# RWKV heads in pairs on whole 128x128 tiles, half of the rate products on GpSimd, and a repeated list schedule with due dates

## The chip, the core and the metric

The kernel runs on one core of a Trainium2 chip. TensorE (PE, with PEld for its weight loads), VectorE (DVE), ScalarE (ACT), GpSimd (POOL) and SyncE (SP, which issues the DMAs) each take their own instructions in order and meet through semaphores. The metric is the device time of one execution in microseconds, the median of several runs.

## The reference

Two layers on 512 positions of 1024 channels, then a final norm. Each layer projects the normed input and feeds three branches: a gated linear recurrence with a short convolution (RG-LRU), an RWKV-7 recurrence with 16 heads of 64 channels, and a retention. The branches are projected back, gated, summed and added to the input. The change is in the RWKV branch, whose core is this recurrence over positions:

```python
kk = kk / jnp.maximum(jnp.linalg.norm(kk, axis=-1, keepdims=True), 1e-12)
k = k * (1.0 + (a - 1.0) * k_a)
def step(state, inp):
    r_t, w_t, k_t, v_t, kk_t, a_t = inp
    sa = jnp.einsum("bhvk,bhk->bhv", state, -kk_t)
    state = (state * w_t[:, :, None, :]
             + sa[..., None] * (kk_t * a_t)[:, :, None, :]
             + v_t[..., None] * k_t[:, :, None, :])
    y = jnp.einsum("bhvk,bhk->bhv", state, r_t)
    return state, y
y = head_norm(y, RWKV_GN_EPS).reshape(bsz, s, W_B) * lnx_w + lnx_b
bonus = (jnp.sum(rh * kh * r_k, axis=-1, keepdims=True) * vh).reshape(bsz, s, W_B)
return (y + bonus) * jax.nn.silu(g)
```

## The kernel before

Channels lie on the 128 partitions, the 512 positions in the columns. A projection (`proj`, L502) streams 282 weight tiles of 128x1024 from HBM (`raw`, 512 KB each). ACT rounds a tile to fp32r (`whi`), DVE makes the remainder (`wlo`), and the product is three matmuls for each of eight slices of the contraction: 24 records named `acc` of 128x128 weights and 512 columns. PSUM buffers of `acc` are freed by the ACT and DVE instructions that read them out.

RWKV works on four groups in each layer, one group being two tiles of 128 channels, that is four heads. For a group, `rwkv_prep` (L749) makes the decays and `rwkv_scores` (L791) the rest: decayed copies of the keys and rates (`ar`, `bk`), the 64x64 products of a chunk with itself (`sc`, one head on a 64-row tile), which DVE masks into `E`. Then a forward elimination on POOL inverts 32x32 triangles (`ex`, `etmp`, 62 instructions of up to 64x256); its input comes by DMA (`ead`) and its result goes out by DMA (`exd`), is transposed by DVE (`xn`), and PE makes the remaining quarter of each inverse (`w`, 32x32 tiles). `vt` are the values transposed, `pcp` the chunk decays.

`rwkv_chain` (L913) goes through eight chunks of 64 positions in turn. A step is a hop from PE to ACT or DVE and back, three times: `p` from the state `sv` (64 columns, weights `ar` and `stk`), copied to `zs` by ACT; `p` from `zs` with weights `E`, copied to `sv`; `p` from `sv` with `tbk`, to which DVE adds the decayed old state (`dec`, made on POOL). All of these are 64x64 or 128x64 tiles. `stk` is `ar` and `E` moved across the partitions by DMA, 256 KB each. `rwkv_out` (L953) norms the result and transposes it back (`yt`).

Nothing is issued where it is written. `Scheduler` records every instruction with a price in us and the tiles it reads and writes, `run` makes a list schedule over the engines from these prices, priorities and free buffers, and then issues in that order. So all rows of the profile have line 318, and work is told apart by its tiles, out<-in. Tiles come from pools with a fixed number of buffers; `etmp`, `sgb`, `g`, `bonus` and `lraw` share the pool `tc` with seven.

## Time and profile before

| | us |
|---|---|
| median of three runs | 2125.97 |
| the runs | 2125.53, 2125.97, 4809.5 |
| span of the profiled execution | 2125.0 |
| PE busy | 2082.5 (98%) |
| DVE busy | 1145.0 (54%) |
| ACT busy | 914.6 (43%) |
| POOL busy | 415.0 (20%) |

The profile is of one execution, whose span is its own time. PE's busy time counts overlapping matmuls once; what one matmul costs is read from one start to the next, since matmuls are pipelined and their ends modelled. PE made 12204 records, DVE 1605 instructions, ACT 1384, POOL 590. The granted clock of PE was 0.9 or more of full speed in nearly all of 40 slices of the span.

### The profile page before, as it was taken

Reading aid. Unit: us, or ns where it says so; the run is one execution under the profiler, and the core shown is the slowest. Engines: PE = TensorE matmul, PEld = TensorE weight load, DVE = VectorE, ACT = ScalarE, POOL = GpSimd, SP = SyncE. Lnnn points to the kernel's source line nnn. Section 1 sums busy time; section 2 is a strip of 40 time slices with the busy share of each in tenths; the row PEclk is TensorE's granted clock in tenths of the full one; section 3 lists DMA queues with packets and bytes.
Section 4 is the critical chain, followed back from the end, with each engine's and each line's share of the span. In section 5 each row is a group of like instructions: output and inputs, shape, how many; then the busy total and the mean of one; then the engine's idle time right before and its main releaser. Section 6 shows DMA issues by size and latency. Waiting matters only on the chain.

```text
span 2125.0 us, 30185 instructions
## 1 busy us (share of the span) xinstructions
PE 2082.5 (98%) x12204; PEld 1648.6 (78%) x12204; DVE 1145.0 (54%) x1605; ACT 914.6 (43%) x1384; POOL 415.0 (20%) x590
## 2 busy tenths in 40 slices
PE   7999999999999999999999999999999999999996
PEld 5777788787788777888877777787887787788884
DVE  8764584474448524344568546644744555253433
ACT  5754652534442424232456466425344424242333
POOL 1062107005200800000010801251070035100000
PEclk9999999999999999999999999999999999999998
DMA  4332242123214323243524212421431243142441
GB/s 161 102 110 63 76 133 89 50 95 102 80 47 128 115 74 124 95 139 99 175 76 131 87 54 92 124 85 54 111 97 55 75 117 122 50 147 92 139 139 60
DMA packets 103147, 210.63 MB, mean 99 GB/s; under 512 B 42848, under 2 KB 44128, under 8 KB 103008
## 3 DMA queue, kind: packets, MB, share of 16 engines
q1 hardware_dynamic: 103008, 208.71, 31.5%
q8 instruction: 96, 1.57, 0.3%
q14 instruction: 43, 0.35, 0.1%
HBM read 175.11 MB, written 20.97 MB: 92 GB/s over the span
## 4 chain that ended last, share of the span: by engine, by line
PE 88%; POOL 5%; DVE 2%; DMA 1%; ACT 1%; issue 1%; SPq 0%; DVEq 0%; ACTq 0%; POOLq 0%
PE acc L318 61%; PE p L318 8%; PE vp L318 5%; PE sc L318 3%; POOL etmp L318 3%; POOL ex L318 3%; PE gate L318 2%; PE w L318 2%; PE rsc L318 2%; PE rout L318 2%; PE lora L318 1%; PE vt L318 1%; PE kss L318 1%; PE tr L318 1%; PE bps L318 1%
## 5 line engine op out<-in xcount | busy, mean ns | idle before, releaser
L318 PE MATMUL acc<-hh,whi 128*128 128x512 f32 x1504 | 621.2, 413 | 2.4 <-DVE q L318 2.4
L318 PE MATMUL acc<-hl,whi 128*128 128x512 f32 x1504 | 590.7, 393 | 3.7 <-DVE hl L318 2.4
L318 PE MATMUL acc<-hh,wlo 128*128 128x512 f32 x1504 | 590.7, 393 | 0.8 <-DVE wlo L318 0.6
L318 DVE TENSOR_TENSOR wlo<-raw,whi 128x1024 fp32r<-128x1024 f32 x282 | 357.7, 1268 | 313.9 <-ACT whi L318 312.2
L318 ACT ACTIVATE whi<-raw 128x1024 fp32r<-128x1024 f32 x282 | 298.0, 1057 | 519.7 <-PE acc L318 367.0
L318 PEld LDWEIGHTS acc<-hh,whi 128*128 128x128 f32 x1504 | 284.0, 189 | 78.7 <-issue 12.3
L318 PEld LDWEIGHTS acc<-hh,wlo 128*128 128x128 f32 x1504 | 284.0, 189 | 64.2 <-DVE wlo L318 2.3
L318 PEld LDWEIGHTS acc<-hl,whi 128*128 128x128 f32 x1504 | 284.7, 189 | 60.2 <-issue 3.4
L318 POOL TENSOR_TENSOR etmp<-ex,ea 64x31 f32<-64x31 f32 (+15 forms) x248 | 169.1, 682 | 131.7 <-DMA ea<-ead 85.4
L318 POOL TENSOR_TENSOR ex<-ex,etmp 64x31 f32<-64x31 f32 (+15 forms) x248 | 167.0, 674 | 19.4
L318 POOL TENSOR_TENSOR dec<-sv,pc 64x256 f32<-64x256 f32 x48 | 51.7, 1077 | 473.1 <-DVE sv L318 473.1
L318 ACT ACT_TABLE_LOAD x87 | 111.6, 1283 | 2.2 <-PEq L1202 0.7
L318 PE MATMUL acc<-yh,whi 128*128 128x512 f32 x256 | 103.0, 402 | 0.0
L318 PE MATMUL acc<-ylo,whi 128*128 128x512 f32 x256 | 100.5, 393 | 0.0
L318 PE MATMUL acc<-yh,wlo 128*128 128x512 f32 x256 | 99.8, 390 | 0.0
L318 ACT ACTIVATE thm<-acc,der 128x512 f32<-128x512 f32 x48 | 33.0, 687 | 137.7 <-PE acc L318 136.9
L318 PE MATMUL acc<-mq,whi 128*128 128x512 f32 x256 | 79.3, 391 | 0.0
L318 PE MATMUL acc<-yq,whi 128*128 128x512 f32 x256 | 78.9, 389 | 0.0
L318 PE MATMUL vp<-whi,hh 128*128 128x256 f32 x256 | 77.7, 304 | 0.0
L318 ACT ACTIVATE zs<-p 64x256 f32<-64x256 f32 x64 | 24.1, 377 | 119.6 <-PE p L318 119.2
L318 POOL TENSOR_TENSOR hl<-hf,hh 128x512 fp32r<-128x512 f32 x8 | 12.8, 1601 | 311.7 <-ACT hh L318 311.7
L318 DVE TENSOR_TENSOR sv<-p,pc 64x256 f32<-64x256 f32 x56 | 23.3, 417 | 93.2 <-PE p L318 79.6
(208 smaller groups left out, 3193.5 us busy)
## 6 DMA issues: line engine op xcount, KB each, us to landing
raw<-in_w SPq DMA_DIRECT2D x282, 512.0 KB, 3.3
yl<-ys SPq DMA_DIRECT2D x48, 256.0 KB, 4.9
stk<-ar SPq DMA_DIRECT2D x16, 256.0 KB, 4.7
ar<-E SPq DMA_DIRECT2D x16, 256.0 KB, 3.0
stk<-E SPq DMA_DIRECT2D x16, 256.0 KB, 3.0
ys<-thg SPq DMA_DIRECT2D x16, 256.0 KB, 2.9
ys<-bonus SPq DMA_DIRECT2D x16, 256.0 KB, 2.3
ys<-yr SPq DMA_DIRECT2D x16, 256.0 KB, 2.6
```

The lines of the kernel that those rows point to most:

```text
L318: fn(*[r(v) for v in pos], **{k: r(v) for k, v in kw.items()})
```

## The change

Two heads share a whole 128x128 tile, one in each half of the partitions, and zeros fill the rest. The score factors become `se` and `so`, the triangles `xd` (both heads on the diagonal) and `br`, the state update `tb`; a chain step has 4 + 2 + 2 + 2 products, with one head's columns in each half of the rows of `sv` and `zs`. The copies of a hop are split, half 0 on ACT and half 1 on DVE. The decay of a chunk is multiplied into `bk` ahead of its transposes, so `pcp` and the moves `stk` are gone. `vt` is made of fp32r halves, `yt` is a product with a constant instead of a transpose, `lraw` is padded to 128 rows, and `w` uses 128x128 weights. Of the rate products, `r * pp` and `k * pi` go to POOL in 64 half products of 64x512; 136 fills with zeros go there too. `raw` has two buffers instead of three, `whi` three instead of two.

The scheduler gets new prices, twelve rounds, and due dates: after a round, the date by which each instruction must start so that PE is not held up, worked back from the round's own times, is the priority in the next; the shortest round is issued. Buffers of the PSUM pools `a` and `d` may be taken out of the recorded order. An argument `claims` is handed through, and emptied where an instruction is committed.

```diff
--- before.py
+++ after.py
-    caps = {"h": 16, "tp": 16, "tc": 7, "tm": 13, "q": 12, "sv": 1, "raw": 3, "whi": 2, "wlo": 2,
-            "zs": 2, "sn": 2, "pc": 2, "ssq": 2, "vm": 2}
+    caps = {"h": 16, "tp": 16, "tc": 7, "tm": 13, "q": 12, "sv": 1, "raw": 2, "whi": 3, "wlo": 2,
+            "zs": 2, "sn": 2, "pc": 2, "ssq": 2, "vm": 2, "vv": 2}
+    S.loose = {"a", "d"}
...
+    def _set_due(self):
+        for op in sorted(self.ops, key=lambda o: (-o.start, -o.i)):
+            due = op.start if op.eng == "PE" or not op.succ else math.inf
+            for s in op.succ:
+                due = min(due, s.due - op.cost - LATENCY[op.eng] * (not s.eng == op.eng == "PE"))
...
+            x = x[:8] + ((),)
...
+    def run(self, rounds=12):
+        for op in self.ops:
+            op.left, op.due = op.ndep, None
+        best = None
+        for _ in range(rounds):
+            length = self._schedule()
+            if best is None or length < best[0]:
+                best = length, sorted(self.ops, key=lambda o: (o.start, o.i))
+            self._set_due()
+        order = best[1]
...
-        c = 0.095 + out.size / 1200.0
+        c = 0.18 + out.size / 1200.0
...
-        S.rec("DVE", nc.vector.tensor_tensor, 0.07 + out.size / 960.0, dict(out=out, in0=in0, in1=in1, op=op))
+        S.rec("DVE", nc.vector.tensor_tensor, 0.15 + out.size / 960.0, dict(out=out, in0=in0, in1=in1, op=op))
...
-    def mm(out, lhsT, rhs, start, stop, n, check=True):
...
-        cost = n / 2400.0 + 0.0025 if fast else max(n, lhsT.size) * 4 / 2400.0
-        if out.box[0]:
-            cost = 0.04
-        S.rec("PE", nc.tensor.matmul, cost, kw, pos=(out,))
+        cost = (n + 32) / 2400.0 if fast else (4 * max(n, 64) + 26) / 2400.0
+        S.rec("PE", nc.tensor.matmul, cost, kw, pos=(out,), claims=claims)
 
     def transpose(out, in_, ident):
-        S.rec("PE", nc.tensor.transpose, 0.06, {}, pos=(out, in_, ident))
+        S.rec("PE", nc.tensor.transpose, 0.109, {}, pos=(out, in_, ident))
...
+        raw = tl("tc", "lraw", [P, 2, 256])
+        memset("POOL", raw[HK:P, 0], 0.0)
+        memset("POOL", raw[0:HK, 1], 0.0)
+        dma(raw[0:HK, 0], wt[l, W_LORA][0:HK, g * 256:(g + 1) * 256], HK * 1024)
+        dma(raw[HK:P, 1], wt[l, W_LORA][HK:P, g * 256:(g + 1) * 256], HK * 1024)
...
-            tt(A[:, :, 0, 1:], c3(kn[:])[:, :, 1:], c3(pp[:])[:, :, :CH - 1], ALU.mult)
-            tt(A[:, :, 1, :], c3(r[i][:]), c3(pp[:]), ALU.mult)
+            for s_, A in enumerate((se, so)):
+                rr = half(s_)
+                stt(A[rr, :, s_, 1:], c3(kn[:])[rr, :, 1:], 2.0, c3(pp[:])[rr, :, :CH - 1], ALU.mult, ALU.mult)
+                ts(A[rr, :, s_, 0:1], c3(kn[:])[rr, :, 0:1], 2.0, None, ALU.mult)
+                ptt(A[rr, :, 1 - s_, :], c3(r[i][:])[rr], c3(pp[:])[rr], ALU.mult)
...
-            tt(B[:, :, 1, :], c3(k[i][:]), c3(pi[:]), ALU.mult)
+            for s_ in range(2):
+                rr = half(s_)
+                tt(B[rr, :, s_, :], c3(kn[:])[rr], c3(pi[:])[rr], ALU.mult)
+                ptt(B[rr, :, 1 - s_, :], c3(k[i][:])[rr], c3(pi[:])[rr], ALU.mult)
...
-                            mm(ps[:, c4, :], B[rr, c].rearrange("p a s -> p (a s)"),
-                               A[rr, c].rearrange("p a s -> p (a s)"), True, True, P)
-                    tt(e[:, 4 * half:4 * half + 4, :], ps[:], mask_s.unsqueeze(1).to_broadcast([P, 4, P]), ALU.mult)
...
+            xd, br = tl("q", "xd", [P, NCH, P]), tl("q", "br", [P, NCH, P])
+            for s_ in range(2):
+                memset("POOL", xd[half(s_), :, half(1 - s_)], 0.0)
+                memset("POOL", br[half(s_), :, half(s_)], 0.0)
+            for hf in range(2):
+                pe, po = tl("rp", "sc", [P, 4, P]), tl("rp", "sc", [P, 4, P])
+                with S.group():
+                    for c4 in range(4):
+                        c = 4 * hf + c4
+                        for s_, (ps, A) in enumerate(((pe, se), (po, so))):
+                            mm(ps[:, c4, :], B[half(s_), c].rearrange("p a s -> p (a s)"),
+                               A[half(s_), c].rearrange("p a s -> p (a s)"), True, True, P)
+                cc = slice(4 * hf, 4 * hf + 4)
+                lo, hi = half(0), half(1)
+                masked(xd[lo, cc, lo], pe[lo, :, lo], m_s, HK)
+                masked(xd[hi, cc, hi], po[hi, :, hi], m_s, HK)
+                masked(br[lo, cc, hi], pe[lo, :, hi], m_i, HK)
+                masked(br[hi, cc, lo], po[hi, :, lo], m_i, HK)
+                tt(se[hi, cc].rearrange("p c a s -> p c (a s)"), pe[hi],
+                   m_si[hi].unsqueeze(1).to_broadcast([HK, 4, P]), ALU.mult)
+                tt(so[lo, cc].rearrange("p c a s -> p c (a s)"), po[lo],
+                   m_is[lo].unsqueeze(1).to_broadcast([HK, 4, P]), ALU.mult)
+            for q in range(4):
...
+            bt = B[:].rearrange("p c a s -> p c (a s)")
+            tt(bt, bt, pc[:, i, :].unsqueeze(2).to_broadcast([P, NCH, P]), ALU.mult)
...
-                        mm(ps[HK:P, c4, :], v[i][:, c * CH:(c + 1) * CH], blkc, True, True, P)
+                        for n, w in enumerate((vh, vl)):
+                            mm(ps[:, c4, :], w[:, c * CH:(c + 2) * CH], blkr[:], n == 0, n == 1, P)
...
-                    mm(ps[32:64, m, :], E[hd][0:32, c, 32:64], xn[0:32, hd, c, :], True, True, 32)
+                    mm(ps[:, i, c, :], XD[i][:, c, :], xn[:, i, c, :], True, True, 32)
...
-                    mm(ps[0:32, m, :], xn[32:64, hd, c, :], E[hd][32:64, c, 32:64], True, True, 32)
+                    mm(ps[:, c], xw[:, i, 32 * c:32 * c + P],
+                       XD[i][:, c, :].rearrange("p (h b t) -> p h b t", h=2, b=2)[:, :, 1, :], True, True, 64)
...
+                for i in range(2):
+                    for s_, A in enumerate((SE[i], SO[i])):
+                        mm(p1[:, cc, i, s_, :], A[:, c].rearrange("p a s -> p (a s)"), sv[:, c, i, s_, :],
+                           cc == 0 and i == 0 and s_ == 0, False, HK, check=False)
+            zs = tl("zs", "zs", [P, 2, HK])
+            act(zs[half(0)], p1[half(0), cc, :, 0, :], ACTF.Copy)
+            vcopy(zs[half(1)], p1[half(1), cc, :, 1, :])
+            if 0 < c < NCH - 1:
+                dec = tl("sn", "dec", [P, 2, HK])
+                for s_ in range(2):
+                    rr = half(s_)
+                    ptt(dec[rr], sv[rr, c, :, s_, :], pc[rr, :, c:c + 1].to_broadcast([HK, 2, HK]), ALU.mult)
+            p2 = tl("rc", "p2", [P, 6, HK])
-                for hd in range(4):
-                    mm(p1[0:HK, c % 2, hd, :], stk[hd][:, c, 0], sv[:, c, hd, :], True, True, HK)
-            with S.group():
-                for hd in range(4):
-                    mm(p1[HK:P, c % 2, hd, :], stk[hd][:, c, 1], sv[:, c, hd, :], c % 2 == 0 and hd == 0, False, HK,
-                       check=False)
-            zs = tl("zs", "zs", [HK, 4, HK])
-            act(zs[:], p1[0:HK, c % 2], ACTF.Copy)
...
-            with S.group():
-                for hd in range(4):
-                    mm(p2[:, 0, hd, :], E[hd][0:HK, c, 0:CH], zs[:, hd, :], True, True, HK)
-            act(sv[0:HK, c], p2[:, 0], ACTF.Copy, scale=-1.0)
+                for i in range(2):
+                    mm(p2[:, i, :], XD[i][:, c, :], zs[:, i, :], True, True, HK)
+            act(sv[half(0), c, :, 0, :], p2[half(0), 0:2, :], ACTF.Copy, scale=-1.0)
+            ts(sv[half(1), c, :, 1, :], p2[half(1), 0:2, :], -1.0, None, ALU.mult, ps=True)
             if c < NCH - 1:
                 with S.group():
-                    for hd in range(4):
-                        mm(p2[:, 1, hd, :], tbk[hd // 2][:, c, (hd % 2) * HK:(hd % 2 + 1) * HK], sv[:, c, hd, :],
-                           True, True, HK)
-                tt(sv[0:HK, c + 1], p2[:, 1], pcb, ALU.mult)
-                if c > 0:
-                    tt(sv[0:HK, c + 1], sv[0:HK, c + 1], dec[:], ALU.add)
+                    for i in range(2):
+                        mm(p2[:, 2 + 2 * i:4 + 2 * i, :], TB[i][:, c, :], sv[:, c, i], True, True, 2 * HK)
+                for s_ in range(2):
+                    rr = half(s_)
+                    if c > 0:
+                        tt(sv[rr, c + 1, :, s_, :], p2[rr, 2 + s_:6:2, :], dec[rr], ALU.add)
+                    else:
+                        vcopy(sv[rr, c + 1, :, s_, :], p2[rr, 2 + s_:6:2, :])
             with S.prio(0.5), S.group():
-                for hd in range(4):
-                    mm(p1[HK:P, c % 2, hd, :], E[hd][0:HK, c, CH:2 * CH], sv[0:HK, c, hd, :], False, True, HK,
-                       check=False)
-            if c % 2 == 1:
+                for i in range(2):
+                    mm(p1[:, cc, i], BR[i][:, c, :], sv[:, c, i], False, True, 2 * HK, check=False)
...
-                        transpose(ps[:, c, :], yn[HK:P, c].rearrange("p h v -> p (h v)"),
-                                  cs[HK:P, C_ID + HK:C_ID + P])
+                        mm(ps[:, c, :], yn[:, c].rearrange("p h v -> p (h v)"), ii, True, True, CH)
```

By the order of instructions PE goes from 9854 matmuls to 9070, DVE from 1607 instructions to 1935, ACT from 1386 to 1449, POOL from 595 to 843, SP from 630 DMAs to 590. Three places show how the order moves.

PE, a step of the first chain before; behind it stand the next projections:

```order
L318 MATMUL p_1837<-zs,E 64x64 [waits Activation_49]
L318 MATMUL p_1837<-zs,E 64x64 x3
L318 MATMUL acc<-hh,whi 128x512
L318 MATMUL acc<-hl,whi 128x512
L318 MATMUL acc<-hh,wlo 128x512
L318 MATMUL acc<-hh,whi 128x512
L318 MATMUL acc<-hl,whi 128x512
L318 MATMUL acc<-hh,wlo 128x512
L318 MATMUL p_1837<-sv,tbk 64x64 [waits Activation_49]
L318 MATMUL p_1837<-sv,tbk 64x64 x3
L318 MATMUL p_1806<-sv,E 64x64 x4
```

PE, the last step of the first chain now (`p_2445` is the output of that chunk):

```order
L354 MATMUL p_2445<-sv,br 128x128 x2
L354 MATMUL p_2445<-sv,se 128x64 [waits DVE_49]
L354 MATMUL p_2445<-sv,so 128x64 [waits DVE_49]
L354 MATMUL p_2445<-sv,se 128x64
L354 MATMUL p_2445<-sv,so 128x64
L354 MATMUL p_2487<-zs,xd 128x64 [waits DVE_49]
L354 MATMUL p_2487<-zs,xd 128x64
L354 MATMUL p_2445<-sv,br 128x128 [waits DVE_49]
L354 MATMUL p_2445<-sv,br 128x128
L354 MATMUL acc<-hh,whi 128x512 [waits DVE_49]
L354 MATMUL acc<-hl,whi 128x512
```

A hop of the chain had four matmuls on 64x64 tiles, with projections ahead of the next one; now it has two on whole tiles, and at the chain's end no projection stands between the hops. The `acc` behind the chain waits for DVE.

DVE at the same place now, the first twelve behind the last `sv` of the first chain (`se`, `so`, `bk` and the rest are the next group's):

```order
L354 TENSOR_REDUCE ssq<-yn 128x8 [waits Activation_49]
L354 SCALAR_TENSOR_TENSOR se<-ksq,pp 64x8x63
L354 SCALAR_TENSOR_TENSOR so<-ksq,pp 64x8x63
L354 TENSOR_SCALAR se<-ksq 64x8
L354 TENSOR_SCALAR so<-ksq 64x8
L354 TENSOR_REDUCE ssq<-yn 128x8 [waits Activation_49]
L354 SCALAR_TENSOR_TENSOR ksq<-lth,ksq 128x512 [waits DVE_49]
L354 TENSOR_SCALAR lth<-lth,der_165 128x512 [waits DVE_49]
L354 TENSOR_TENSOR bk<-ksq,pi 64x8x64
L354 TENSOR_TENSOR k<-k,lth 128x512 [waits DVE_49]
L354 TENSOR_TENSOR bk<-ksq,pi 64x8x64
L354 SCALAR_TENSOR_TENSOR r<-r,par_146,k 128x512 [waits DVE_49,Pool_49]
```

Before, the next group's factors stood behind the chain too, with more instructions of other work between them; now they stand close together, ahead of the read-out of the next `acc`.

ACT at the third group's elimination before (`xn<-w` is work on the elimination's result):

```order
L318 ACTIVATE sgb<-g 128x512 [waits DVE_49]
L318 ACTIVATE g<-acc,der_133 128x512 [waits PE_49]
L318 ACTIVATE whi<-raw 128x1024 [waits DMAHW6_49]
L318 ACTIVATE sgb<-g 128x512 [waits DVE_49,Pool_49]
L318 ACTIVATE whi<-raw 128x1024 [waits DMAHW7_49,PE_49]
L318 ACTIVATE xn<-w_4703 32x512 [waits PE_49]
L318 ACTIVATE E<-w_4735 32x8x32 [waits PE_49]
```

and now:

```order
L354 ACTIVATE lwh<-lraw 128x512 [waits DMAHW2_49,DMAHW4_49,DVE_49,Pool_49]
L354 ACTIVATE whi<-raw 128x1024 [waits DMAHW5_49,PE_49]
L354 ACTIVATE zs<-p_4789 64x128 [waits PE_49]
L354 ACTIVATE sgb<-g 128x512 [waits DVE_49,Pool_49]
L354 ACTIVATE whi<-raw 128x1024 [waits DMAHW6_49,PE_49]
L354 ACTIVATE whi<-raw 128x1024 [waits DMAHW7_49,DVE_49,PE_49]
```

The second `sgb` of the group, which waits for POOL, now stands ahead of a run of `whi`, behind the `zs` of a chain that is still running.

## Rows read from the trace of the kernel before

**Rows 1.** The page: span, busy time by engine, two costly groups, the weight load.

```profile
span 2125.0 us, 30185 instructions
...
PE 2082.5 (98%) x12204; PEld 1648.6 (78%) x12204; DVE 1145.0 (54%) x1605; ACT 914.6 (43%) x1384; POOL 415.0 (20%) x590
...
L318 POOL TENSOR_TENSOR dec<-sv,pc 64x256 f32<-64x256 f32 x48 | 51.7, 1077 | 473.1 <-DVE sv L318 473.1
...
raw<-in_w SPq DMA_DIRECT2D x282, 512.0 KB, 3.3
```

**Rows 2.** What PE waited for: us in total, times, longest us.

```profile
PE w L318 <- DVE xn L318: 7.0, 4, 3.3
```

**Rows 3.** The chain of waits: start us, us, what.

```profile
by line: PE acc L318 60.9%; PE p L318 7.9%; PE vp L318 4.5%; PE sc L318 2.9%; POOL etmp L318 2.7%; POOL ex L318 2.6%; PE gate L318 1.8%; PE w L318 1.7%; PE rsc L318 1.7%; PE rout L318 1.6%; PE lora L318 1.2%; PE vt L318 1.1%; issue 1.1%; PE
...
106.56 1.64 PE sc L318 x16
...
825.31 232.78 PE acc L318 x1026
```

**Rows 4.** Timeline of PE, 101.6 to 105.3 us: start us, us, instruction.

```profile
101.67 0.39 PE L318 MATMUL acc<-hh,wlo 128*128 128x512 f32 x1
101.90 0.60 PE L318 MATMUL tr<-cs,bk 128*128 128x128 f32 x4
102.25 0.48 PE L318 MATMUL acc<-hh,whi 128*128 128x512 f32 x1
102.56 0.39 PE L318 MATMUL acc<-hl,whi 128*128 128x512 f32 x1
...
103.49 0.40 PE L318 MATMUL acc<-hh,wlo 128*128 128x512 f32 x1
103.82 1.16 PE L318 MATMUL sc<-ar,bk 64*128 64x128 f32 x8
104.90 0.50 PE L318 MATMUL acc<-hh,whi 128*128 128x512 f32 x1
105.24 0.39 PE L318 MATMUL acc<-hl,whi 128*128 128x512 f32 x1
```

**Rows 5.** Timeline of PE, 226 to 240 us, a step of a chain.

```profile
228.49 0.68 PE L318 MATMUL p<-zs,E 64*64 64x64 f32 x8
229.10 0.50 PE L318 MATMUL acc<-hh,whi 128*128 128x512 f32 x1
```

**Rows 6.** Groups of instructions, shapes apart: busy us, mean ns; weight loads.

```profile
L318 PEld LDWEIGHTS sc<-ar,bk 64*128 64x128 f32 x512 | 58.5, 187 | 13.5 <-issue 7.2 <-DVE E L318 1.5 <-DVE wlo L318 1.4
...
L318 PEld LDWEIGHTS w<-xn,E 32*32 32x32 f32 x512 | 18.9, 113 | 12.3 <-issue 10.2 <-DVE xn L318 1.0 <-PE acc L318 0.7
```

**Rows 7.** Timeline of PEld, 101.6 to 105.3 us.

```profile
102.22 0.19 PEld L318 LDWEIGHTS acc<-hh,whi 128*128 128x128 f32 x1
102.33 0.19 PEld L318 LDWEIGHTS acc<-hl,whi 128*128 128x128 f32 x1
```

**Rows 8.** Timeline of PE, 489 to 491.5 us: third group's last scores.

```profile
488.88 2.05 PE L318 MATMUL sc<-ar,bk 64*128 64x128 f32 x16
```

**Rows 9.** Timeline of POOL, 542 to 546 us: end of its elimination.

```profile
543.84 0.60 POOL L318 TENSOR_TENSOR ex<-ex,etmp 64x31 f32<-64x31 f32 x1
```

**Rows 10.** Groups of DVE and ACT, shapes apart: busy us, mean ns.

```profile
L318 DVE TENSOR_TENSOR wlo<-raw,whi 128x1024 fp32r<-128x1024 f32 x282 | 357.7, 1268 | 313.9 <-ACT whi L318 312.2 <-DMA ead<-E 0.4 <-DMA xr<-in_x 0.2
...
L318 DVE TENSOR_TENSOR E<-sc,cs 128x512 f32<-128x512 f32 x64 | 43.5, 684 | 19.4 <-PE sc L318 19.2
...
L318 ACT ACTIVATE E<-p 64x128 f32<-64x128 f32 x128 | 24.6, 269 | 37.2 <-PE p L318 37.0
...
L318 DVE TENSOR_TENSOR sv<-p,pc 64x256 f32<-64x256 f32 x56 | 23.3, 417 | 93.2 <-PE p L318 79.6 <-ACT thm L318 13.1
```

**Rows 11.** Timeline of ACT, 226 to 233 us: a copy of a chain.

```profile
229.26 0.38 ACT L318 ACTIVATE sv<-p 64x256 f32<-64x256 f32 x1 [0.22 <-PE p L318]
```

**Rows 12.** Busy by stretch: us, busy of each engine, PEclk, DMA share.

```profile
177.70:184.00 6.30, 6.22 (x42) 5.31 (x43) 4.86 (x8) 0.59 (x1) 0.00 (x0) 0.50 0.60 149
```

More of the change, by code (lines that the diff above doesn't have):

```diff
@@ L208, in _commit, with _use @@
         self.ops.append(op)
-    def _access(self, op, ap, write, deps):
-        t, b = ap.t, ap.box
-        if not t.log:
+    def _use(self, op, t):
+        if t.first is None:
             op.allocs.append(t)
@@ L227, in _access, with _schedule @@
             t.log.append((False, b, op))
-    def run(self):
+    def _set_due(self):
+        takers = {}
+        for ts in self.fifo.values():
+            for t in ts:
+                if t.before is not None:
+                    takers.setdefault(id(t.before), []).append(t.first)
+        for op in sorted(self.ops, key=lambda o: (-o.start, -o.i)):
+            due = op.start if op.eng == "PE" or not op.succ else math.inf
+            for s in op.succ:
+                due = min(due, s.due - op.cost - LATENCY[op.eng] * (not s.eng == op.eng == "PE"))
+            for t in op.tiles:
+                for s in takers.get(id(t), ()):
+                    if s.due is not None and s.start > op.start:
+                        due = min(due, s.due - op.cost - LATENCY[op.eng])
+            op.due = due
+    def _schedule(self):
         engines = ("PE", "ACT", "DVE", "POOL", "SP")
@@ L249, in slot_time @@
                 n = want.get(k, 0)
-                f = self.fifo[k]
-                if nxt[k] + n >= len(f) or f[nxt[k] + n] is not t or n >= len(free[k]):
+                f = left_of[k]
+                if n >= len(free[k]) or (t.pool not in self.loose and (n >= len(f) or f[n] is not t)):
                     return None
-                when = max(when, sorted(free[k])[n])
+                when = max(when, sorted(x[0] for x in free[k])[n])
                 want[k] = n + 1
@@ L294, in run @@
             op.start, op.done = st, st + cost + LATENCY[e]
-            order.append(op)
             left -= 1
             for t in op.tiles:
-                t.users -= 1
+                t.left -= 1
                 t.free_at = max(t.free_at, op.done)
-                if t.users == 0:
-                    free[t.pool, t.tag].append(t.free_at)
+                if t.left == 0:
+                    free[t.pool, t.tag].append((t.free_at, left, t))
             for s in op.succ:
@@ L310, in run @@
                     pend[s.eng].append(s)
-        order.sort(key=lambda o: (o.start, o.i))
+        return max(o.done for o in self.ops)
+    def run(self, rounds=12):
[8 more added lines that the diff above has]
+        order = best[1]
         def r(v):
@@ L318, in run @@
                 fn(*[r(v) for v in pos], **{k: r(v) for k, v in kw.items()})
-        return max(o.done for o in order)
+        return best[0]
 @with_exitstack
@@ L666, in retention @@
         vp = [tl("a", "vp", [P, 2, 256]) for _ in range(2)]
+        vs = [tl("tm", "vc", [P, 2, 256]) for _ in range(2)]
         for half in range(2):
@@ new lines, in rwkv_scores @@
+        for i in range(2):
+            for q in range(4):
+                p0, rr = 32 * i + 8 * q, slice(32 * q, 32 * q + 32)
+                dma(XD[i][rr, :, rr], exd[p0:p0 + 8].rearrange("c s t -> s c t"), 32768, small=True)
+        xn, xw = tl("tc", "xn", [P, 2, NCH, 32]), tl("q", "xw", [P, 2, 352])
+        memset("POOL", xw[:], 0.0)
+        for q in range(2):
+            memset("POOL", xn[HK * q + 32:HK * q + 64], 0.0)
+            rr = slice(HK * q, HK * q + 32)
+            for i in range(2):
+                S.rec("DVE", nc.vector.transpose, 0.43, dict(out=xn[rr, i], in_=XD[i][rr, :, rr]))
```

361 lines of the change are left out of this document (177 added, 184 removed).

## The prediction

> **What bounds the kernel now.** First the page: PE is busy in 98% of the span, DVE in 54%, ACT in 43%, POOL in 20% [rows 1]. Next the table of who PE waited for: it adds up to 25.0 us, and one row lies at this change's place, 7.0 us in four waits of the `w` products for `xn` [rows 2]. So PE is fed almost always, and the time is the sum of what its instructions take from one start to the next. The chain of waits gives that, since where the chain stays on one engine a piece lasts from start to start [rows 3]: 1026 projection records (`acc`, 512 columns) take 232.78 us, 0.227 each. By its line of shares `p` has 7.9%, `sc` 2.9%, `w` 1.7% and `lora` 1.2% of 2125 us: 168, 62, 36 and 25.5 us. The 128 `yt` transposes, at the 0.06 us that 64-column records take below, add 8. Together 300 us. (An fp32 product is two records, one of fp32r or a transpose is one.)
>
> Then the timeline, where small matmuls meet projections [rows 4]. From 101.67 to 102.56 run two projections and four transposes on the whole array: 0.89 us, less two projections 0.44, 0.11 per transpose and nothing for the change of work. Eight `sc` records on a 64-row tile are different: the projection ahead holds PE 0.33 us (103.49 to 103.82), the one behind 0.34 (104.90 to 105.24), not 0.227. **A change of tile size costs** 0.10 + 0.11 us. In PE's order before, 296 stretches of smaller tiles stand between whole-array work.
>
> **What the change removes.** 32 such stretches are left, all `sc`. The projections around the other 264 get back 0.21 us each: **-55 us**. The small records' own side of these borders is in the 300 us. Also gone are 48 transfers of 256 KB, which PE hid (nothing), and 32 `pcp` matmuls, 4 us.
>
> **What PE does instead.** All new small records load 128 columns of weights. What limits a 64-column product behind such a load is not in the trace, so it is bounded. Loads of 32 and 128 columns last 113 and 187 ns [rows 6], and two 128-column loads in a row start 0.11 us apart (102.22, 102.33) [rows 7]: I take 0.11 us per record. The lower end is 64-column products as they run now, 0.61 us for eight (228.49 to 229.10) [rows 5], less the border 0.06. The Trainium skill ("TensorE: Matmul & The Clock Gate", section "LDWEIGHTS (loading the stationary operand)") says that a load takes its columns divided by 1.2 GHz: an estimated 107 ns for the change's loads where the old took 53, which speaks against packing two heads side by side; the rows agree.
>
> Counts from the order: the chain has 1248 records, 137 us instead of 168. `sc` has 32 stretches of 16 that alternate between the row halves; two heads that met before overlapped, 16 records in 1.64 us [rows 3] against 2 x 1.08 alone [rows 4]. With full overlap 8 x 0.11 + 0.20 each, 35 us for 62; without any, 63. I take overlap, as every record has a partner. `w`: 512 records, 56 for 36. `yt`, now a product: 256, 28 for 8. `lora`: 96 whole-array records, 22 for 25.5. `vt` loads 128 columns before and after, 256 records: nothing. Sum 278 against 300 and 4: **-26 us**.
>
> **What the new order makes PE wait for.** This is new, and the order shows where; each place comes once per layer, so twice.
> - *The third elimination.* `sgb` takes its buffer in the same pool of seven as the elimination's `etmp`, and in ACT's new order it waits for POOL with three `whi` right behind it; before, it stood just ahead of the elimination's result. The elimination ends 53.5 us after the last scores of its tile (490.93 to 544.44) [rows 8, 9], then come `sgb` and its product, near 0.68 each as other work on 512 columns, and the `wlo` behind them, 1.27 [rows 10]: 56.1 us. Between the last scores and the projection that needs this `wlo`, PE has 80 `acc` (18.2 us), 96 `vp` (4.5% of the span for 768, so 12.0), 32 `vt` (3.5) and 24 others (some 5): 39 us. It waits 17: **+34 us**. Were POOL's products ahead of the elimination late by 3 us, 40.
> - *The fourth scores.* From the first `wlo` of that place to its last mask product DVE has 50 instructions: 5 of 1024 columns, 27 of 504 or 512, 16 of 256, two small. At 1.27, 0.68 and 0.417 us [rows 10] that is 31.7 us in a queue that PE's `sc`, `tr` and `acc` wait for piece by piece, and PE's own work there is 44 `acc`, 64 `sc` and 16 transposes, 16.1 us. **+31 us**; 16 if DVE runs half of it ahead.
> - *Behind the first chain.* Right behind its last products stands a projection that needs a free PSUM buffer, which DVE frees with its 14th instruction from there: twelve of about 0.68 us and two small ones [rows 10], 8.5 us. **+17 us**; 0 if PE comes late.
> - *Hops without cover.* In the last three steps of the fourth chain and the last of the first, 11 hops have no other PE work between product, copy and product. A copy of 128 columns takes 0.27 us [rows 10], and one began 0.22 us after PE's last record [rows 11]; with as much on the way back 0.7 us each: 22 hops, **+15 us** (11 with nothing on the way back).
> - *Behind the last chain* 18 projections (4.1 us) stand ahead of `yt`, whose way is some ten instructions of ACT and DVE of 0.27 to 0.68 us, with hand-overs near 7 us: **+6 us**.
>
> After the 3.3 us wait for `xn` PE ran 6.3 us at a granted clock of 0.50, its 1.2 GHz level [rows 12], which costs half, 3.2 us. Four places of each layer hold PE for as long or longer (all but the hops): **+26 us**. The two old ones go, for there are now 306 projection records (69 us) between a layer's last first scores and its first `w`, where there were 240: -7 and -6, **-13 us**.
>
> **Other engines.** DVE's 328 further instructions at 0.71 us [rows 1] bring it to 64%, no bound in total; the places above are where its queue is. POOL gets 64 half products of 512 columns and 136 fills: `dec` takes 1.08 us on the mean for 256 [rows 1], so up to 2.2 us each, hidden except as said. With `raw` two deep a weight tile has 2 x 24 x 0.227 = 10.9 us for load, `whi` and `wlo`; 3.3 for the load and 1.27 for `wlo` [rows 1, 10] leave `whi` 6 us, so this is hidden.
>
> 2125 - 55 - 26 + 34 + 31 + 17 + 15 + 6 + 26 - 13 = **2160 us**. The profiled span, 2125.0 us, stands 1 us below the median shown, 2125.97.
>
> **Rivals.**
> A, loads cost nothing extra: 64-column products follow at 0.06 us. Then 1536 records lose 0.05 us each (-77) and `vt` 13: 2070 us; where PE waits anyway, about a sixth of it comes back as wait: 2085. For it: a `w` load lasts 113 ns and `w` records, 36 us for 1024, take 0.035, so loads do run ahead of their products. Against it: the 0.11 us between loads. Chance 0.20. By the skill ("TensorEngine Tiling (Array Packing)", section "Instruction Overhead") a matmul has a fixed overhead of about 60 cycles, and the page names no cost for a load's width; that would be this rival, and the load rows stand against it.
>
> B, slower: the clock does not come back between the waits. In the fourth scores and the fourth chain's tail PE works in pieces of some us between waits; if all that work, 16 and some 12 us per layer, and the 5 us behind it run at 0.50, another 2 x 24 = 48 us or so go beyond what the sum has: 2208. From 4 us more per layer than I have put in, the time is over 2% worse. For it: 6.3 us of full work at 0.50 followed one 3.3 us wait. Against it: where waits are under 1 us, as at the hops, the trace before has no such stretch. Chance 0.28.
>
> C, the waits are shorter because the engines run ahead of where the counts put them: a third of the 103 us goes, 2126; it is inside the forecast.
>
> **How the numbers follow.** The forecast has 0.52, A 0.20, B 0.28. Its own range comes from the bounds: the waits -35 or +15, scores without overlap +28, a border of 0.18 or 0.24 +-8: 2120 to 2195. To hold 8 in 10 it goes down to A and most of the way to B: 2085 to 2205. A measurement of this kernel can tell 2%, 43 us, from no change: under 2083 is faster, over 2168 slower. Of A about half is faster, and a little of the forecast's lower end; of B nearly all and a quarter of the forecast are slower: faster 0.13, same 0.50, slower 0.37.
>
> **What would show it.** Right: `acc` beside `p`, `w`, `vt` at 0.23 us, beside `sc` at 0.33; chain records 0.11 us apart; 16 `sc` in 1.1 us; PE's waits near 120 us, the longest, 17 us, twice, for a `wlo` behind the third elimination; clock rows of 0.50 after them. Wrong: 0.06 us between chain records (A); waits under 60 us in all, or none at `sgb`, would refute the second half and leave a gain of some 80 us; `acc` at 0.33 beside whole-array fp32 records would refute the border term and take the time to 2215.

## The result and the profile after

The changed kernel takes 2222.92 us (2221.63 to 2230.95), the kernel before 2127.13 us beside it: a ratio of 1.0459 with a 95% interval from 1.0439 to 1.048. The ratio is one of fast runs, so it leaves out the run of 4809.5 us that is in the median of the kernel before. The change is slower by 4.6%. The forecast was 2160 us with a range up to 2205: the direction was right, the time 63 us too short.

The page of the changed kernel, its span and busy times, answers to [rows 1]:

```profile
span 2221.2 us, 27634 instructions
PE 2062.3 (93%) x10508; PEld 1707.0 (77%) x10508; DVE 1291.1 (58%) x1933; ACT 922.4 (42%) x1447; POOL 562.2 (25%) x838
```

PE is busy for 20 us less and its span is 96 us longer. Three pieces make that up. Idle time is the span less PE's busy time: 42.6 us before, 158.9 now. Time at a granted clock of 0.50 is 36 us before, 207 now, of which PE works in 19.4 and 113.7; work at 0.50 is taken here to need twice its time, so that half of it is lost, 9.7 and 56.8 us. What is left is PE's work at full speed, 2072.7 and 2005.5 us.

| us | before | after | difference | forecast |
|---|---|---|---|---|
| PE's work at full speed | 2072.7 | 2005.5 | -67 | -81 |
| PE idle | 42.6 | 158.9 | +116 | +96 |
| lost to work at 0.50 | 9.7 | 56.8 | +47 | +20 |
| span | 2125.0 | 2221.2 | +96 | +35 |

Whom PE waited for in the changed kernel (us in total, times, longest us), which answers to [rows 2]:

```profile
PE acc L354 <- DVE wlo L354: 36.6, 6, 16.4
PE acc L354 <- DVE k L354: 27.8, 2, 13.9
PE acc L354 <- ACT xh L354: 9.6, 1, 9.6
PE tr L354 <- DVE br L354: 8.1, 4, 2.9
PE p L354 <- DVE sv L354: 7.5, 10, 0.8
PE sc L354 <- POOL bk L354: 7.0, 4, 2.6
PE acc L354 <- DVE ylo L354: 6.4, 2, 3.2
PE acc L354 <- ACT yq L354: 6.1, 2, 3.1
PE p L354 <- DVE zs L354: 5.8, 8, 0.8
...
PE yt L354 <- DVE yn L354: 3.4, 4, 1.0
```

The table adds up to 141 us, and the old row of `w` waiting for `xn` is gone. The 16.4 us stand behind the third elimination, 13.9 behind the first chain, `tr`, `sc` and `ylo` are the fourth scores, `sv` and `zs` the hops without cover, `yq` the projections behind the last chain; each place comes once per layer. `yt` waits behind the second and third chains only. ACT's timeline shows the first of them: the second `sgb` stood idle for 25.85 us until the elimination's last `ex`, and PE's timeline what hangs on it (start us, us, instruction, idle before and its releaser):

```profile
591.69 0.63 ACT L354 ACTIVATE sgb<-g 128x512 f32<-128x512 f32 x1 [25.85 <-POOL ex L354]
```

```profile
594.23 0.79 PE L354 MATMUL acc<-hh,wlo 128*128 128x512 f32 x1 [16.39 <-DVE wlo L354]
594.83 0.63 PE L354 MATMUL acc<-hh,whi 128*128 128x512 f32 x1
595.25 0.63 PE L354 MATMUL acc<-hl,whi 128*128 128x512 f32 x1
595.68 0.63 PE L354 MATMUL acc<-hh,wlo 128*128 128x512 f32 x1
```

The projections behind the wait start 0.42 us apart, not 0.227: that is the low clock. The busy times by stretch (the columns of [rows 12]) show it at all four places of the first layer:

```profile
280.70:297.80 17.10, 4.79 (x11) 3.80 (x12) 16.82 (x19) 6.45 (x10) 13.42 (x15) 0.50 0.00 0
581.10:598.20 17.10, 3.97 (x9) 3.14 (x10) 5.75 (x8) 2.06 (x3) 9.61 (x22) 0.50 0.13 36
738.10:768.80 30.70, 22.39 (x95) 16.45 (x94) 19.66 (x32) 10.02 (x21) 12.52 (x22) 0.61 0.17 55
874.60:898.50 23.90, 17.17 (x57) 14.31 (x58) 8.06 (x18) 11.36 (x26) 3.39 (x8) 0.50 0.11 34
```

The first column after the length is PE busy. Behind the two long waits there is little work in the slow stretch, 4 to 5 us; in the fourth scores and from the tail of the fourth chain on PE works for most of it, 18 and 17 us at 0.50.

PE's timeline around small products, where they do have cover, answers to [rows 4, 5]:

```profile
866.02 0.33 PE L354 MATMUL p<-sv,se 128*128 128x64 f32 x2
866.19 0.39 PE L354 MATMUL p<-sv,so 128*128 128x64 f32 x2
866.41 0.39 PE L354 MATMUL p<-sv,se 128*128 128x64 f32 x2
866.63 0.39 PE L354 MATMUL p<-sv,so 128*128 128x64 f32 x2
866.83 0.48 PE L354 MATMUL acc<-hh,whi 128*128 128x512 f32 x1
...
868.07 0.39 PE L354 MATMUL acc<-hh,wlo 128*128 128x512 f32 x1
868.30 0.55 PE L354 MATMUL p<-zs,xd 128*128 128x64 f32 x4
868.66 0.48 PE L354 MATMUL acc<-hh,whi 128*128 128x512 f32 x1
868.98 0.39 PE L354 MATMUL acc<-hl,whi 128*128 128x512 f32 x1
```

Two records of 64 columns take 0.22 us, 0.11 each. The projection ahead of `p` takes 0.23 (868.07 to 868.30), as forecast; the one behind still takes 0.32 (868.66 to 868.98).

### The profile page after: what moved, and what is told of

Its sections match the earlier page's. It is cut to its first block, busy times and chain, and to the rows that moved or that the text cites. A ratio compares the mean times of both kernels' runs of the same rounds, so it can differ in the third digit from the quotient of the medians.

```text
span 2221.2 us, 27634 instructions
## 1 busy us (share of the span) xinstructions
PE 2062.3 (93%) x10508; PEld 1707.0 (77%) x10508; DVE 1291.1 (58%) x1933; ACT 922.4 (42%) x1447; POOL 562.2 (25%) x838
## 5 line engine op out<-in xcount | busy, mean ns | idle before, releaser
L354 PE MATMUL acc<-hh,whi 128*128 128x512 f32 x1504 | 614.3, 408 | 33.4 <-DVE k L354 27.8
L354 PEld LDWEIGHTS acc<-hh,wlo 128*128 128x128 f32 x1504 | 286.1, 190 | 101.7 <-DVE wlo L354 39.5
L354 POOL TENSOR_TENSOR etmp<-ex,ea 64x31 f32<-64x31 f32 (+15 forms) x248 | 153.1, 617 | 133.6 <-DMA ea<-ead 112.9
L354 POOL TENSOR_TENSOR dec<-sv,pc 64x128 f32<-64x128 f32 x96 | 43.6, 454 | 564.0 <-DVE sv L354 560.4
L354 POOL TENSOR_TENSOR bk<-k,pi 64x512 f32<-64x512 f32 x32 | 54.4, 1701 | 149.1 <-issue 78.0
L354 PE MATMUL acc<-yq,whi 128*128 128x512 f32 x256 | 84.4, 411 | 7.9 <-ACT yq L354 6.1
L354 PE MATMUL vp<-whi,hl 128*128 128x256 f32 x256 | 72.6, 284 | 0.0
L354 PE MATMUL vp<-wlo,hh 128*128 128x256 f32 x256 | 72.5, 283 | 0.0
```

What stands on the lines that cost most here:

```text
L354: fn(*[r(v) for v in pos], **{k: r(v) for k, v in kw.items()})
```

## The experiments

All runs stand beside runs of the kernel before on the same chip. In the table, waits is the sum of the waits table, and the last three columns are the pieces of the table above. These four come from the profile of each run, whose time lies up to 12 us from the median (e7_old_plan: 2154.63).

| run | us | ratio to before (95%) | waits | PE idle | lost at 0.50 | PE's work |
|---|---|---|---|---|---|---|
| the change | 2222.92 | 1.0459 (1.0439 to 1.048) | 141 | 159 | 57 | 2005 |
| e1_fill | 2224.85 | 1.0444 (1.0423 to 1.0465) | 98 | 116 | 54 | 2054 |
| e2_etmp_own | 2185.06 | 1.0267 (1.0252 to 1.0282) | 105 | 122 | 61 | 2002 |
| e3_pool_low_raw3 | 2150.97 | 1.0105 (1.0087 to 1.0122) | 82 | 100 | 50 | 2000 |
| e4_due_before | 2137.61 | 1.0043 (1.002 to 1.0066) | 30 | 48 | 17 | 2068 |
| e5_fill_chain | 2223.88 | 1.0448 (1.0424 to 1.0472) | 136 | 154 | 51 | 2020 |
| e6_rates_dve | 2227.47 | 1.0479 (1.0456 to 1.0502) | 145 | 163 | 55 | 2009 |
| e7_old_plan | 2167.0 | 1.0196 (1.0175 to 1.0218) | 102 | 120 | 28 | 2005 |
| e8_pool_high | 2305.81 | 1.0841 (1.0824 to 1.0857) | 180 | 198 | 98 | 2009 |
| e9_old_plan_etmp | 2126.42 | 0.9991 (0.998 to 1.0003) | 64 | 82 | 36 | 2004 |
| e10_one_round | 2218.6 | 1.0427 (1.0414 to 1.0441) | 134 | 150 | 57 | 2009 |
| e11_pool_low | 2193.01 | 1.0301 (1.0283 to 1.0318) | 106 | 124 | 56 | 2002 |
| e12_claims | 2263.69 | 1.0639 (1.061 to 1.0669) | 161 | 179 | 74 | 2008 |
| e13_fill_all | 2215.12 | 1.0415 (1.04 to 1.0431) | 89 | 106 | 33 | 2074 |
| e14_raw3 | 2238.93 | 1.0518 (1.0501 to 1.0536) | 147 | 164 | 76 | 2001 |

**Is the wait behind the third elimination a shared buffer's?** The order is kept; `etmp` gets a buffer of its own, and `zs` has one buffer instead of two to make room.

```diff
-            self._real = p.tile(list(self.shape), self.dtype, tag=self.tag, name=self.name)
+            own = self.name == "etmp"
+            if own:
+                p = self.sch.pools["et"][0]
+            self._real = p.tile(list(self.shape), self.dtype, tag="et" if own else self.tag, name=self.name)
...
-        S.add_pool(n, ctx.enter_context(tc.tile_pool(name=n, bufs=b)), b)
+        S.add_pool(n, ctx.enter_context(tc.tile_pool(name=n, bufs=1 if n == "zs" else b)), b)
+    S.pools["et"] = (ctx.enter_context(tc.tile_pool(name="et", bufs=1)), None)
...
-        tmp = tl("tc", "etmp", [64, 512])
+        tmp = tl("tc", "etmp", [64, 256])
```

> The changed kernel with the same order; only the buffer of etmp is its own (1 KB, 64x256) instead of one of the seven that sgb shares, and zs has one buffer instead of two to make room. Theory (the wait behind the third elimination is a shared buffer's): sgb waits for POOL no longer, the two 16.4 us waits for wlo go and most of the slow stretch behind them, time down by 30 to 42 us, 2181 to 2193. Rival (that place is bound by DVE or by weights anyway): the wait comes back under another name and the time stays over 2210.

2185.06 us, 38 less. The 16.4 us waits are gone from the table, the 13.9 us ones stand as they were. The theory holds, with its size. In the kernel's order this `sgb` is the seventh tile that the pool gives out behind `etmp`, and the pool has seven buffers: the planner gives a tile any buffer that is free, while in the kernel the buffers come in turn.

**Does the packed work make the waits, or the order?** Two runs change one price of the plan and no instruction, one of them the buffers of `raw` too:

```diff
-        S.rec("POOL", nc.gpsimd.tensor_tensor, 0.32 + out.size / 480.0, dict(out=out, in0=in0, in1=in1, op=op))
+        S.rec("POOL", nc.gpsimd.tensor_tensor, 0.12 + out.size / 455.0, dict(out=out, in0=in0, in1=in1, op=op))
...
-    caps = {"h": 16, "tp": 16, "tc": 7, "tm": 13, "q": 12, "sv": 1, "raw": 2, "whi": 3, "wlo": 2,
+    caps = {"h": 16, "tp": 16, "tc": 7, "tm": 13, "q": 12, "sv": 1, "raw": 3, "whi": 2, "wlo": 2,
```

> The changed kernel's instructions, all of them on the same engines; only the plan is made with POOL products priced at 0.12 us + columns / 455 instead of 0.32 + columns / 480 (the trace says 0.62 to 0.70 us for 256 columns, so the new price is the truer one), and raw has three buffers, whi two. Theory (the loss is the order's waits and the clock behind them, and the packed work itself gains some 67 us): waits fall below 80 us, half-speed time below 100 us, time 2085 to 2130, no slower than before. Rival (the packed work is slower by itself, since DVE has 328 more instructions and POOL's products slow it): time stays over 2180 whatever the order.

2150.97 us: 72 less than the change, but short of what I expected, and still 1% over the kernel before. Half-speed time is 134 us where I had put under 100, and other waits have come, 18.4 us of `yt` for `yn` among them.

```diff
-        S.rec("POOL", nc.gpsimd.tensor_tensor, 0.32 + out.size / 480.0, dict(out=out, in0=in0, in1=in1, op=op))
+        S.rec("POOL", nc.gpsimd.tensor_tensor, 0.5 + out.size / 480.0, dict(out=out, in0=in0, in1=in1, op=op))
```

> The changed kernel's instructions and nothing changed but one price of the plan: POOL products at 0.50 + columns / 480 instead of 0.32. Theory (the loss lies in how the order spreads projections, and a plan that believes in longer eliminations puts more projections there and fewer beside the chains): time over 2250, waits over 165 us, the added waits at chains and behind them. Rival (the price of a POOL product has little to do with it): within 1% of 2223.

2305.81 us, 83 more, with 180 us of waits. The hops show best what became thinner: `p` waits for `sv` 24 times and for `zs` 18 times, where the change has 10 and 8.

```profile
PE acc L354 <- DVE wlo L354: 35.6, 7, 14.4
PE acc L354 <- DVE k L354: 26.1, 4, 7.4
PE p L354 <- DVE sv L354: 18.8, 24, 1.3
PE tr L354 <- DVE bk L354: 17.9, 6, 4.2
PE p L354 <- DVE zs L354: 17.1, 18, 2.0
```

With `0.1 + out.size / 455.0` for the same price and nothing else changed:

> The change with only the plan's price of a POOL product put back to 0.1 + columns / 455; raw and whi as in the change. It tells the two edits of the earlier run apart. Theory: the price alone brings most of that run's 72 us, so 2150 to 2180. If the buffers of raw and whi were what helped, over 2200.

2193.01 us, 30 less, and 13 above the range: the price alone does not bring most of the 72. And `raw` alone, `"raw": 3, "whi": 2` under the price of the change:

> The change with three buffers for raw and two for whi as before, planned anew, and the high POOL price kept. If a short weight queue is what costs (I had put it at nothing), the time falls by about the 42 us that lie between the two runs with the low price, to 2170 to 2195. If those 42 us came from another order that happened to fit better, it stays within 2200 to 2245.

2238.93 us, 16 more. So under this price three buffers for `raw` bring nothing. The 42 us between the two runs with the low price stay open: they differ in these buffers, by 0.02 us in the price, and through both in the order. Where no fillers (below) are added, PE's work is 2000 to 2009 us in all orders of the new work. What moves is the rest.

**Which part of the new planner?** The plan of before for the new work (`rounds=1`, all prices of before), then the same order with `etmp` in its own buffer as above:

```diff
-    def run(self, rounds=12):
+    def run(self, rounds=1):
...
-        c = 0.18 + out.size / 1200.0
+        c = 0.095 + out.size / 1200.0
...
-        cost = (n + 32) / 2400.0 if fast else (4 * max(n, 64) + 26) / 2400.0
+        cost = n / 2400.0 + 0.0025 if fast else max(n, lhsT.size) * 4 / 2400.0
```

> The changed kernel's instructions with the plan made in one round without due dates and with all the prices of before. Theory (the packed work gains some 67 us, the order of this change loses it): waits between those of before (25 us) and of the change (145), time 2110 to 2200. Rival (the packed work itself makes the waits, whatever the plan): over 2205.

2167.0 us, inside the range of the theory. Behind its longest wait, 21.4 us for `wlo`, stands the same `sgb`:

```profile
567.70 0.63 ACT L354 ACTIVATE sgb<-g 128x512 f32<-128x512 f32 x1 [25.91 <-POOL ex L354]
```

> The kernel of the run with the old plan (same order) with etmp in a buffer of its own and zs with one. In that run PE's waits for wlo are 44 us in four, the longest 21.4. If they are the shared buffer again, as in the order of the change, they go and the time falls by 40 to 60 us to 2105 to 2127, no slower than the kernel before; if they have another cause, it stays near 2167.

2126.42 us, 41 less, and level with the kernel before. The same `sgb` now follows the work ahead of it without idle time:

```profile
542.58 0.62 ACT L357 ACTIVATE sgb<-g 128x512 f32<-128x512 f32 x1
```

This is the best of the runs with the packed work, and no gain: 69 us less work for PE pay for 40 us more of idle time and 26 more of work at 0.50.

One round with the new prices (`rounds=1` alone), due dates for the old work (the change's `Scheduler` in the kernel before), and claims that are kept (the line `x = x[:8] + ((),)` taken out):

> The change with one round of planning, so without due dates, and everything else as it is, the new prices too. If the due dates and the further rounds are to blame for the order, the time falls clearly below 2200; if the prices and the new work are, it is 2205 to 2245.

> The kernel before with nothing changed but the scheduler: twelve rounds with due dates, its own old prices and its own work. If due dates are what spoils the order, this is slower than before by 20 us or more. If the loss belongs to the new work together with the new prices, it is the same as before, 2110 to 2135.

> The change with the one line gone that empties claims, so that a projection takes its read-out buffer in the plan when it takes its PSUM bank. If the emptied claims are what makes PE run ahead of the read-out and wait behind the first chain, that wait (2 x 13.9 us) goes and the time falls by 20 to 40 us; if claims only bind the plan further, the time is the same or up to 60 us longer.

2218.6, 2137.61 and 2263.69 us. Due dates neither cause the loss nor bring anything: with them the old work is slower by 0.4%, 10 us, which is 3 above the range for no effect and half of what I had put for blame, and the new one by 0.2%, with intervals that overlap. Claims make it longer by 41 us. The wait behind the first chain does go with them, and 39.5 us of `acc` for `whi` and 22.5 of `sc` for `bk` come. It is gone in e3_pool_low_raw3, e7_old_plan and e11_pool_low too, where claims are emptied as in the change, so this run does not show that the emptied claims cause it.

**The rates back on DVE**, in the order of the change:

```diff
-        S.rec("POOL", nc.gpsimd.tensor_tensor, 0.32 + out.size / 480.0, dict(out=out, in0=in0, in1=in1, op=op))
+        S.rec("POOL", (nc.vector if out.t.name in ("se", "so", "bk") else nc.gpsimd).tensor_tensor, 0.32 + out.size / 480.0, dict(out=out, in0=in0, in1=in1, op=op))
```

> The changed kernel with the plan of the change and only the 64 half products of the rates issued on DVE instead of POOL, at the places that the plan gave them. DVE gets 64 x 0.69 = 44 us, POOL loses 64 x 1.70 = 109. If DVE's queue is the bound at the fourth scores and behind the first chain, the time rises by 15 to 44 us, 2235 to 2265, since most products stand at the scores. If POOL's slow products (1.70 us) are what PE waits for, it falls by 5 to 20.

2227.47 us, the same within the intervals. Neither side was right: DVE's longer queue and POOL's slow products cost PE the same. The reason stands in DVE's timeline behind the first chain of the change, with POOL's beside it:

```profile
282.67 1.13 DVE L354 TENSOR_SCALAR se<-ksq 64x8 f32<-64x8 f32 x1
...
285.34 1.56 DVE L354 TENSOR_SCALAR lth<-lth,der 128x512 f32<-128x512 f32 x1
...
287.43 0.67 DVE L354 TENSOR_TENSOR k<-k,lth 128x512 f32<-128x512 f32 x1
288.13 0.69 DVE L354 TENSOR_TENSOR bk<-ksq,pi 64x512 f32<-64x512 f32 x1
288.86 1.64 DVE L354 SCALAR_TENSOR_TENSOR r<-r,par,k 128x512 f32<-128x512 f32 x1
290.53 1.64 DVE L354 TENSOR_TENSOR yn<-xd,ssq 64x512 f32<-64x512 f32 x1
292.20 0.75 DVE L354 SCALAR_TENSOR_TENSOR k<-acc,par,k 128x511 f32<-128x511 f32 x1
```

```profile
282.04 1.74 POOL L354 TENSOR_TENSOR se<-r,pp 64x512 f32<-64x512 f32 x1
...
285.36 1.26 POOL L354 TENSOR_TENSOR so<-r,pp 64x512 f32<-64x512 f32 x1
...
288.19 3.43 POOL L354 TENSOR_TENSOR bk<-k,pi 64x512 f32<-64x512 f32 x2 [0.82 <-DVE k L354]
```

While POOL makes two `bk` products, two of DVE's instructions with two SBUF inputs take 1.64 us instead of some 0.7. Over the span `r<-r,par,k` has a mean of 743 ns before and 1052 now. The run with the products on DVE shows the same place without them on POOL:

```profile
287.37 0.75 DVE L354 TENSOR_SCALAR lth<-lth,der 128x512 f32<-128x512 f32 x1
...
291.52 0.74 DVE L354 SCALAR_TENSOR_TENSOR r<-r,par,k 128x512 f32<-128x512 f32 x1
292.27 0.69 DVE L354 TENSOR_TENSOR yn<-xd,ssq 64x512 f32<-64x512 f32 x1
```

There DVE is busy for 1294.1 us in all, with 64 instructions more than in the change, where it has 1291.1. What DVE gains by giving 0.69 us away it loses to the neighbour. The Trainium skill ("GPSIMD Engine Reference", section "1. Specifications") says that POOL's interfaces to SBUF are shared with VectorE, with contention where DVE has two SBUF inputs or runs in a 2-port perf mode. The rows of `r` and `yn`, with two inputs, agree; `se` and `lth` have one, and no row shows their mode.

**Does the low clock cost time by itself?** PE gets further matmuls with zero weights in its waits, added to a projection that is open, so the output is the same and the order too:

```diff
+        fill = {2481: 62, 3053: 4, 3057: 2, 3065: 12, 3067: 9, 3068: 2, 3089: 10, 3093: 2, 7015: 62, 7587: 4, 7591: 2, 7599: 12, 7601: 9, 7602: 2, 7623: 10, 7627: 2}
+        count, open_ = 0, {}
...
+                if op.eng == "PE":
+                    count += 1
+                    for _ in range(fill.get(count, 0) if open_ else 0):
+                        out, rhs = list(open_.values())[-1]
+                        self.nc.tensor.matmul(out, lhsT=zero, rhs=rhs, start=False, stop=False)
```

> The changed kernel, same order, with 206 further PE matmuls of 512 columns and zero weights added to a projection that is already open, put ahead of eight waiting instructions of each layer: 62 ahead of the wlo wait behind the third elimination (16.4 us), 41 ahead of the waits in the fourth scores (12 us together). They should lie inside the waits. If the low clock behind the waits costs time by itself (47 us of half-speed loss in the trace of the change, about 11 us of it per layer at these two places), the rows of 0.50 there go and the time falls by 10 to 22 us, 2200 to 2212. If DVE or POOL sets the pace there and PE at half speed is hidden, the rows of 0.50 go and the time stays at 2217 to 2228. If the low clock has nothing to do with standing still, the rows stay.

2224.85 us: no difference. The stretch behind the third elimination runs at 0.90 instead of 0.50, the fourth scores at 0.78 instead of 0.61:

```profile
581.10:598.20 17.10, 14.61 (x58) 11.61 (x57) 5.89 (x8) 2.02 (x3) 9.54 (x21) 0.90 0.13 36
738.10:768.80 30.70, 25.85 (x119) 19.45 (x117) 19.11 (x31) 10.00 (x21) 11.29 (x21) 0.78 0.16 52
```

But it was mostly idle time that left the low clock, and little work: in the first layer 3.4 us of work behind the elimination still run at 0.50 (3.9 in the change) and 13.2 in the fourth scores (18.4), and the loss by the decomposition is 54 us against 57. So the run says little of what slow work costs. Where some of it went, at the fourth scores, the projections behind come within 0.3 us of where they did, counted from those ahead, so nothing was won there. In the fourth chain's tail the fillers go into the bank of the projection that follows, two ahead of each of seven hops and ten ahead of the projection:

> The changed kernel, same order, with 24 zero-weight matmuls of 512 columns in each layer's fourth-chain tail: two ahead of each of seven waiting hops (0.45 us in waits of 0.7 to 0.8) and ten ahead of the 3.1 us wait behind them, into the PSUM bank of the projection that follows. In the trace of the change PE works 17 us per layer at a granted clock of 0.50 there. In this tail each hop waits for PE and PE for each hop, so if the low clock costs anything anywhere it is here: with the clock kept at 1.0 the time falls by up to 2 x 8 us, 2205 to 2212. If the rows of 0.50 stay because the fillers do not keep the clock, 2219 to 2230; if they go and the time stays, the clock costs nothing here either.

2223.88 us, again none. The rows show why (from 871.30 the tail, from 895.50 the `yt` behind it):

```profile
871.30:888.60 17.30, 14.56 (x84) 10.43 (x82) 5.36 (x15) 5.92 (x19) 2.12 (x5) 1.00 0.09 32
895.50:905.70 10.20, 9.73 (x38) 8.65 (x38) 4.96 (x8) 1.49 (x3) 0.00 (x0) 0.50 0.05 19
```

The tail kept its clock and became 4 us shorter, and the clock fell behind it, where PE has 9.7 us of work, half of which is lost. `yt` in the change and in this run:

```profile
899.68 3.75 PE L354 MATMUL yt<-cs,yn 128*128 128x64 f32 x32
```

```profile
895.87 7.06 PE L375 MATMUL yt<-cs,yn 128*128 128x64 f32 x32 [1.58 <-DVE yn L375]
```

It starts 3.8 us earlier and ends 0.5 us earlier. Here the low clock does cost time by itself. So both fills were put together, with eight more ahead of the last `yt` and twelve instead of ten ahead of the tail's projection:

> The change, same order, with zero-weight matmuls in all the places where a projection's bank can be had: the third elimination, the fourth scores, the fourth chain's tail as before, and eight more ahead of the last yt. If half-speed work on PE's own path is what the 47 us of the decomposition are, the clock now stays up from the chain's tail through yt, and the 4 us per layer that the tail won stay won: 2205 to 2216. If the low clock only takes time that other engines hold anyway, the time stays at 2218 to 2228.

2215.12 us, inside the first range: 8 less than the change, and the intervals are apart. Time at 0.50 went from 207 to 107 us, and the loss by the decomposition from 57 to 33. Of 24 us that stood there as loss, 8 came back as time. By the starts of the same instructions in both traces 7 of them lie between the last hops of the two fourth chains and `yt`, 4.1 and 3.0, where the loss was 8.6 each. The fillers are work too, 69 us of it for 53 us less idle time, so the 8 us are what is left after them and not the clock's whole price. Now the tail and what follows run at full clock:

```profile
874.60:898.50 23.90, 21.56 (x121) 16.67 (x121) 12.33 (x24) 12.93 (x28) 3.38 (x8) 1.00 0.11 34
```

## Why the prediction was wrong

The sum was 63 us short, and the result lies 18 us above the range. Two terms had the wrong mechanism, the border and the clock, and the wait behind the first chain had the wrong size. The rest holds: the order of instructions did show where PE would stand still, and each place is in the trace.

- **The border, -55.** This step failed in half. The projection ahead went from 0.32 to 0.23 us as forecast, the one behind only from 0.34 to 0.32. The rows of before had it: behind four transposes on the whole array the projection at 102.25 takes 0.31 us to 102.56 [rows 4]. I spread that over the transposes' own price and called the change of work free. What the projection behind pays belongs to the fp32 work ahead of it, not to the tile. 264 x (0.09 + 0.02) = 29 us. Summed from start to start, slow work at half, `acc` fell by 31 us; the small products that I had in the sum fell by 24 where I had 26. PE's work in all fell by 67 where I had 81, and it is that near only because `kss`, `rout` and `vp`, which I had not in the sum, gave another 12: that part is luck.
- **The loads, 0.11 us per record.** Right; rival A is out. The overlap of the halves of `sc` is right too: the first pair starts at 125.97 on both halves in the trace of the change.
- **The third elimination, 2 x 17.** Right: 16.4 each, and 38 us by the run with its own buffer.
- **The hops, 15.** Right: `p` waits for `sv`, `zs` and, in a row not shown, `sv` of ACT sum to 14.8 us.
- **Behind the first chain, 2 x 8.5.** It was 13.9 each. DVE began with it after an idle 2.3 us, for `yn` of ACT, and its instructions took 12.2 us and not 8.5. Of the 3.7 us, 3.6 are what `se`, `lth`, `r` and `yn` take longer than in e6_rates_dve, where no POOL product lies beside them; I had costed the products on POOL alone.
- **The fourth scores and behind the last chain, 31 and 6.** Some 25 and 6 by the waits table. The 6 are luck: the projections that I had put ahead of `yt` waited 3.1 us for `yq`, and `yt` behind them, at 899.68, did not wait. All these places together are 107 us where the sum had 103; the rest of the 20 us by which idle time was short lies in waits that it did not have, 9.6 us of `acc` for `xh` the longest.
- **The clock, +26 - 6.** This is the largest miss, 27 us in the decomposition. I gave each stop 3.2 us from one row of before. In the decomposition its price is not per stop: it is half of the work that PE does until the clock is back, and that is 4 us behind the third elimination, 18 in the fourth scores, and 17 from the fourth chain's tail on, where short waits go on and the clock stays low. That was rival B, at 2208 the nearest of the cases; I gave it 0.28. Nor does all of it come back: the fills took away 24 us of the loss and won 8, and how much of the rest went into the fillers themselves is not known. So a decomposition into idle and slow work tells where to look, not what each part would give back.
- **Costed at nothing:** the due dates, rightly, and `raw` with two buffers, where PE's table of waits has no row for `whi` in the change; what the buffers do to the order is not told apart.

Open is what the clock costs at the place behind the first chain, where no bank is free for a filler; it was not tried.

## What to carry to other kernels

A change that gives PE less work in a kernel that PE bounds at 98% moves the question to who feeds PE: some 67 us, 64 to 73, were real in every order, and the orders that came with them added 66 us (e9_old_plan_etmp) to 243 us (e8_pool_high) of idle time and slow work. Read the new order of the waiting engines before the run, price each place without cover with the time of all engines that are busy there together, and put the clock's price at up to half of the work that follows until the waits end. A plan's truer price is not a better plan: over POOL's products in the trace of the change, 469 us, the price of the change makes 486 and the low one 356, and the low one gave the faster order. One long-lived tile in a pool that the planner sees as free, while the buffers come in turn, was worth 38 us.

## What the runs showed that I had not expected

- The whole-array fp32 products, `p`, `w`, `yt` and the transposes alike, leave the projection behind them at 0.31 to 0.32 us instead of 0.227; a 64-row or 64-column tile adds 0.02 to that.
- POOL's half products of 64x512 take 1.48 to 1.70 us on the mean and lengthen DVE instructions beside them from some 0.7 to 1.64 us; moved to DVE they change the time by nothing that can be measured.
- Short waits were enough for PE to lose its clock: in the fourth chain's tail, where no wait is over 0.82 us up to 889.4, the clock fell at 874.6 and the 14.8 us in between ran at 0.50, with PE busy in 11.1 of them. With fillers in the hops the tail ran at 1.00.
- The same instructions took 2126 to 2306 us, by the plan's prices and rounds and where one tile lies (and one buffer less for `zs`).
